# Scores in two visits a unit, meta tokens side by side, another product order in the pair stage of a hybrid mixer block

## The chip, the cores and the metric

The kernel runs on one core of a Trainium2 chip. The metric is the device time of one execution in microseconds, as the median of several runs. A profile of one execution gives the busy time and the waits of each engine: TensorE (PE, with its weight loads as PEld), VectorE (DVE), ScalarE (ACT), GpSimd (POOL) and SyncE (SP), which issues the transfers.

## The reference

A block over 1024 tokens and 16 meta tokens, width 1024, in float32: a pooling mixer and a chunked gated linear attention (gla) side by side, merged by gates, then a squared-ReLU MLP. What the change touches is the projection `z = u @ w_in` and the attention:

```python
z = jnp.einsum('bld,dn->bln', u, w_in)
a, q, k, v, r, lr, ga, gb = jnp.split(z, IN_SPLITS, axis=-1)   # 512, 256, 256, 512, 512, 16, 1024, 1024
...
def gla_chunk_step(S, inp):          # a chunk is 64 tokens, 4 heads, DK 64, DV 128
    qc, kc, vc, ac = inp
    b = jnp.cumsum(ac, axis=2)
    decay = jnp.exp(-jnp.abs(b[:, :, :, None, :] - b[:, :, None, :, :]))
    scores = jnp.einsum('bhtk,bhsk,bhtsk->bhts', qc, kc, decay)
    o = jnp.einsum('bhts,bhsv->bhtv', scores, vc) + jnp.einsum('bhtk,bhkv->bhtv', qc * jnp.exp(b), S)
    ...
```

The 16 meta tokens are a leading partial chunk; their keys and values give the first state S.

## The kernel before

Each float32 operand of a large product is split into a high and a low part (`w1h`, `w1l` of a weight, `th`, `tl` of the tokens), and a product of four row blocks is 12 matmuls: high by high (L300), low by high (L301), high by low (L302). ACT makes the high part (L982), DVE the low one (L983). A float32 matmul shows as one row in the profile if its parts are of the split kind, and as two if both operands are plain float32.

The program runs through stages. The first makes the values v (`v_half`, token blocks t = 0 to 7, and t = 8 for the meta tokens, 16 rows). A second makes the first projections in a written order. The third, `pairs_of_projections`, makes the columns of q, gb, ga and r as 11 pairs of 128 columns, by a scheme with 7 products instead of 8 (P1 to P7). Then come the attention across chunks (`across`), the gated output and the MLP.

A pair's products work on quarter blocks of the weights a11, a12, a21, a22 and sums of them that POOL adds (`fs`, `s3`). P1 and P2 add up in one PSUM bank (the x sum), P5 and P3 in another (the z sum); P6, P7 and P4 have banks of their own (`y`). ACT or DVE read the banks out: P1 to `u2p` (ACT, L1094); P2 to the result of the column by `put`, which is a copy or a tanh on ACT (L942; for gb and ga) and for r a tanh, a scaling (L952) and a product on DVE (L953) that reads the bank too; P6 into `u2p`, P7 into `u3p` and then z + `u3p` (L1102), P4 + `u3p` (L1112), P3 as z + `u2p` (L1116), on DVE. `pairs_order` gives the order of the products: P6 of the pair before, P1, P7 of the pair before, P5, then P4 of the pair before, P2, P3 of the pair before. The x sums lie in turns in the two halves (one bank each) of a wide tile `sc`, and the z sums in two tiles `z`. PE follows the order in which the code is written; the order on DVE and ACT is a scheduler's, and waits between engines are semaphores set by which tile an instruction reads or writes.

Between the products stands the inside of the attention, a generator `insides` that is advanced by a credit: four units (two halves of the tokens, two pairs of heads). A unit (`inside`) loads keys, queries and decays into `gi` and `g`, grows them level by level (`grow`, 5 levels, DVE and ACT), and forms 7 score sets of 16 matmuls of 64x64 (the chunk's own and levels 0 to 5). A burst of those between two products is called a visit here. The scores land in halves of a wide tile `gs` and are laid into `gi` with a mask (`inlay`, L1255); the result is stored to `gi_dram`. In the first half of the tokens each unit is followed by `meta_state`, which turns the decayed meta keys and multiplies them with the meta values (`vm`). In `across`, scores times values (L1449) and queries times states (L1459) are two visits each half, with a small copy between (L1454).

Of the kernel before, what the change touches and what calls it, by code (L numbers as in the profile page):

```python
# [14 lines left out]
P = 128  # L15
# [5 lines left out]
CH = 64  # L21
# [9 lines left out]
MP = 264  # L31
PACE, LEVEL, OPENING, STRETCH = 1.3, 1.6, 6.0, 1.9

# [89 lines left out]
def kernel(  # L123
# [154 lines left out]
    def transposed(u, half, at, tags=("ms",), to=None):  # L278
        rows = u.shape[0]
        th, tl = (t[half] for t in to or (TH, TL))  # L280
        if rows == P:
            for j in range(2):
                turn_n[0] += 1
                b = bank(tags[turn_n[0] % len(tags)]).rearrange("p (a b) -> p a b", a=4)
                for i in range(4):
                    pe.transpose(b[:, i], u[:, (4 * j + i) * P : (4 * j + i + 1) * P], ident)
                split_from_psum(th[:, 4 * j : 4 * j + 4, at : at + P], tl[:, 4 * j : 4 * j + 4, at : at + P], b)
                c = half * HALF + at - OFF[half]
                act.activation(S["xr"][:, 4 * j : 4 * j + 4, c : c + P], b, ACT.Copy)
        else:  # L290
            b = bank("ms")[:, : 8 * rows].rearrange("p (a b) -> p a b", a=8)
            for i in range(8):
                pe.transpose(b[:, i], u[:, i * P : (i + 1) * P], ident[:rows, :rows])
            split_from_psum(th[:, :, at : at + rows], tl[:, :, at : at + rows], b)

# [120 lines left out]
    def v_out(i, t):  # L416

        n = P if t < 8 else META
        b = v_bank.pop((i, t))[:n]
# [9 lines left out]
    def lr_turn():  # L429
# [5 lines left out]
        b = two("y2")[:, 0]  # L435
        pe.transpose(b[:16, :16], S["lrtok"][:16, 8], ident[:16, :16])
        stacked(S["lr"][:, SEQ : SEQ + META], b[:16, :16])
# [155 lines left out]
    def start():  # L593
# [412 lines left out]
    def pairs_order(n_pairs):  # L1006
        yield from (("P1", 0), ("P4", 0), ("P2", 0), ("P5", 0))
        for i in range(1, n_pairs + 1):
            for p in ("P6", "P1", "P7", "P5", "P4", "P2", "P3"):
                n = i if p in ("P1", "P5", "P2") else i - 1  # L1010
                if n < n_pairs and (p, n) != ("P4", 0):
                    yield p, n

    def sums_weights(order, n_pairs, load, eng):

        def tt(out, a, b, op):
            for k in (slice(0, 2), slice(2, 4)) if eng is pool else (slice(0, 4),):
                eng.tensor_tensor(out[:, k], a[:, k], b[:, k], op)

        for p, i in order(n_pairs):  # L1020
# [28 lines left out]
    def first_pair():  # L1049
# [5 lines left out]
        w1_slots()  # L1055
        S["pw"] = sums_weights(pairs_order, len(PAIRS), load_pair, pool)

# [4 lines left out]
    def pairs_of_projections():  # L1062
# [5 lines left out]
        S["u2p"] = right.push("u2p", [P, 2, HALF], F32)  # L1068
        S["u3p"] = right.push("u3p", [P, 2, HALF], F32)
        load(1, 0)  # L1070
        load(1, 1)
        S["N"] = [right.push(f"n{i}", [P, HALF, 2], F32) for i in range(2)]
        S["F"] = right.push("f", [P, HALF, 2], F32)
        S["ends"] = right.push("ends", [P, HALF], F32)
        S["g"] = right.push("g", [P, HALF], F32)
        S["gi"] = right.push("gi", [P, 3, HALF], F32)
        banks(keep=1, y=2, gs=1, z=2)
        x, xb, zb = S["xs"], {}, {}
        total = 7 * len(PAIRS)
        chain, credit = insides(), 0.0  # L1080
        for n, (p, i, (ah, al)) in enumerate(ahead(pair_weights(), 3)):
            bh, bl = x[p]
            if p in ("P1", "P2"):
                b = xb[i] = bank("sc") if p == "P1" else xb[i]
            elif p in ("P5", "P3"):
                b = zb[i] = bank("z") if p == "P5" else zb[i]
# [4 lines left out]
            u2, u3 = S["u2p"][:, i % 2], S["u3p"][:, i % 2]  # L1091
            put, d = PAIRS[i][1:]
            if p == "P1":
                act.activation(u2, b, ACT.Copy)  # L1094
            elif p == "P2":
                put(d, 0, xb.pop(i), None)
            elif p == "P6":
                dve.tensor_tensor(u2, b, u2, ALU.add)
            elif p == "P7":
                dve.tensor_tensor(u3, b, u2, ALU.add)  # L1100
                c = nxt("c")
                dve.tensor_tensor(c, zb[i], u3, ALU.add)  # L1102
# [63 lines left out]

    def meta_state(p):
        pre, suf, y, km = (metab[:, i] for i in (META_LOG[p], 1, 2, 4))
        nc.sync.dma_start(km, k_dram[p, :, :META])
        dve.memset(suf, 0.0)  # L1170
        for m in (1, 2, 4, 8):
            twice(pre, suf, m)
        act.activation(y, suf, ACT.Exp, scale=1.0 / TAU)
        dve.tensor_tensor(y, y, km, ALU.mult)
        yield 5.0
        b = two("gs")[:, 0]
        pe.transpose(b[:META, :P], y, ident)
        kt = gB[32 : 32 + META, 2 * 256 : 2 * 256 + P]
        dve.tensor_copy(kt, b[:META, :P])
        yield 2.0  # L1180
        b = two("gs")[:, 0]
        for e in range(2):
            r = slice(e * CH, (e + 1) * CH)
            pe.matmul(
                b[r, :P], kt[:, r], vm[:, (2 * p + e) * P : (2 * p + e + 1) * P], start=True, stop=True,
                tile_position=(32, e * CH),
            )
        dve.tensor_copy(S["S"][:, 0, p], b[:, :P])
# [19 lines left out]
    def inside(p, half):  # L1208
# [42 lines left out]

        yield 2.0

        def inlay(lvl, b):
            dve.copy_predicated(scc, mask[:, lvl : lvl + 1, None, :].broadcast_to([P, 2, 4, CH]), b)  # L1255

        b = [scores(kq[:, 0], kq[:, 1]), scores(N[0][:, :, 0], N[0][:, :, 1])]
        act.activation(scc, b[0], ACT.Copy)
        inlay(0, b[1])
        e, at = g, 0  # L1260
        for lvl in range(6):
            m, n = 1 << lvl, N[lvl % 2]
            to = at + HALF // (2 * m)
            e2 = ends[:, at:to] if lvl < 5 else dec_of(p, half)
            if lvl < 5:
                grow(m, n, N[1 - lvl % 2], e, e2)
            e2_of, e, at = (e, e2), e2, to
            if lvl < 5:
                yield LEVEL
            if lvl in (1, 3):  # L1270
                b = [scores(N[i][:, :, 0], N[i][:, :, 1]) for i in (1, 0)]
                for i in range(2):
                    inlay(lvl + i, b[i])
            elif lvl == 5:
                b = scores(n[:, :, 0], n[:, :, 1])
                last(n, *e2_of)
                inlay(5, b)
        yield LEVEL
# [137 lines left out]
    def across(p, half):  # L1416
# [533 lines left out]
```

## Time and profile before

| | |
|---|---|
| median of 3 runs | 1198.33 us (1198.26 to 1198.54) |
| profiled execution | 1198.67 us, of which the span from first to last instruction is 1195.8 |
| PE busy | 1182.6 us, 99% |
| DVE, ACT, POOL busy | 853.6, 579.0, 102.1 us |
| first stage (values) | 0 to 72.4 us |
| first projections | 72.4 to 140.7 us |
| pair stage | 140.7 to 376.6 us |
| across chunks | 376.6 to about 460 us |

A row of the profile's timeline reads: start in us, duration in us, engine, line, operation, names (out<-in), shape, count, and in brackets the engine's idle time before it and what ended it. PE's rows overlap: a matmul's duration includes its way through the array, and starts of neighbouring products' matmuls are 0.23 us apart.

### The profile page before, as it was taken

Reading aid. Unit: us, or ns where it says so; the run is one execution under the profiler, and the core shown is the slowest. Engines: PE = TensorE matmul, PEld = TensorE weight load, DVE = VectorE, ACT = ScalarE, POOL = GpSimd, SP = SyncE. Lnnn points to the kernel's source line nnn. Section 1 sums busy time; section 2 is a strip of 40 time slices with the busy share of each in tenths; the row PEclk is TensorE's granted clock in tenths of the full one; section 3 lists DMA queues with packets and bytes.
Section 4 is the critical chain, followed back from the end, with each engine's and each line's share of the span. In section 5 each row is a group of like instructions: output and inputs, shape, how many; then the busy total and the mean of one; then the engine's idle time right before and its main releaser. Section 6 shows DMA issues by size and latency. Waiting matters only on the chain.

```text
span 1195.8 us, 18439 instructions
## 1 busy us (share of the span) xinstructions
PE 1182.6 (99%) x6823; PEld 982.5 (82%) x6823; DVE 853.6 (71%) x1400; ACT 579.0 (48%) x1006; POOL 102.1 (9%) x121
## 2 busy tenths in 40 slices
PE   9999999999999999999999999999999999999997
PEld 7999887777778887888788888888888888888886
DVE  7679657565676779527986766777675887887686
ACT  7566544444456224216754555545454444445454
POOL 0224232333220000000000000000000000000000
PEclk9999999999999999999999999999999999999999
DMA  8232533434357879712254544445389963333532
GB/s 247 69 89 81 180 112 113 143 125 142 124 168 265 293 229 306 257 34 89 89 185 143 165 146 163 153 139 167 132 285 336 328 213 97 97 97 97 168 97 88
DMA packets 151001, 192.79 MB, mean 161 GB/s; under 512 B 12088, under 2 KB 85616, under 8 KB 150912
## 3 DMA queue, kind: packets, MB, share of 16 engines
q1 hardware_dynamic: 150752, 191.56, 50.1%
q8 instruction: 53, 0.87, 0.3%
q14 instruction: 36, 0.29, 0.1%
q10 hardware_dynamic: 160, 0.07, 0.0%
HBM read 128.66 MB, written 62.93 MB: 160 GB/s over the span
## 4 chain that ended last, share of the span: by engine, by line
PE 69%; DVE 3%; issue 1%; ACT 1%; DMA 0%; DVEq 0%
PE b_oa L300 5%; PE b_oa L302 5%; PE b_oa L301 5%; PE b_y L300 4%; PE b_mm L300 4%; PE b_y L301 4%; PE b_y L302 4%; PE b_mm L302 4%; PE b_mm L301 4%; PE b_ob L300 4%; PE b_ob L302 4%; PE b_ob L301 4%; PE b_z L301 3%; PE b_z L300 3%; PE b_z L302 3%; PE b_sc L300 2%
## 5 line engine op out<-in xcount | busy, mean ns | idle before, releaser
L300 PE MATMUL b_z<-th,w1h 128*128 128x512 f32 x240 | 94.3, 393 | 0.0
L301 PE MATMUL b_z<-tl,w1h 128*128 128x512 f32 x240 | 93.6, 390 | 0.4 <-DVE tl L1617 0.4
L302 PE MATMUL b_z<-th,w1l 128*128 128x512 f32 x240 | 93.5, 390 | 0.0
L982 ACT ACTIVATE w1h<-raw 128x512 fp32r<-128x512 f32 x103 | 64.0, 622 | 54.9 <-PE b_y L301 23.1
L300 PE MATMUL b_sc<-th,w1h 128*128 128x512 f32 (+1 forms) x232 | 89.8, 387 | 0.7 <-ACT u2p L1733 0.7
L301 PE MATMUL b_sc<-tl,w1h 128*128 128x512 f32 (+1 forms) x232 | 89.2, 385 | 0.0
L302 PE MATMUL b_sc<-th,w1l 128*128 128x512 f32 (+1 forms) x232 | 89.0, 383 | 0.0
L983 DVE TENSOR_TENSOR w1l<-raw,w1h 128x512 fp32r<-128x512 f32 x103 | 70.6, 686 | 18.4 <-ACT w1h L982 18.4
L982 ACT ACTIVATE w1h<-fs 128x512 fp32r<-128x512 f32 x81 | 51.1, 631 | 65.8 <-PE b_y L301 34.2
L983 DVE TENSOR_TENSOR w1l<-fs,w1h 128x512 fp32r<-128x512 f32 x81 | 56.2, 694 | 21.8 <-ACT w1h L982 21.6
L982 ACT ACTIVATE w1h<-bt 128x512 fp32r<-128x512 f32 x46 | 29.1, 632 | 70.8 <-issue 43.9
L1809 DVE TENSOR_TENSOR bt<-w,w 128x512 f32<-128x512 f32 x80 | 54.6, 683 | 0.6 <-DMA w<-in_w_ff_dram 0.6
L301 PEld LDWEIGHTS b_z<-tl,w1h 128*128 128x128 f32 x240 | 45.1, 188 | 9.9 <-DVE tl L1617 0.8
L300 PEld LDWEIGHTS b_z<-th,w1h 128*128 128x128 f32 x240 | 45.0, 188 | 9.8 <-issue 0.2
L302 PEld LDWEIGHTS b_z<-th,w1l 128*128 128x128 f32 x240 | 45.1, 188 | 9.7
L300 PEld LDWEIGHTS b_sc<-th,w1h 128*128 128x128 f32 x232 | 43.6, 188 | 10.4 <-ACT u2p L1733 1.2
L302 PEld LDWEIGHTS b_sc<-th,w1l 128*128 128x128 f32 x232 | 43.6, 188 | 8.8
L301 PEld LDWEIGHTS b_sc<-tl,w1h 128*128 128x128 f32 x232 | 43.6, 188 | 8.6
L300 PE MATMUL b_mm<-wo,th 128*128 128x512 f32 x128 | 50.4, 393 | 0.0
L983 DVE TENSOR_TENSOR w1l<-bt,w1h 128x512 fp32r<-128x512 f32 x46 | 31.7, 690 | 25.6 <-ACT w1h L982 25.6
L302 PE MATMUL b_mm<-wo,tl 128*128 128x512 f32 x128 | 49.9, 390 | 0.0
L301 PE MATMUL b_mm<-wo,th 128*128 128x512 f32 x128 | 49.8, 389 | 0.0
(535 smaller groups left out, 3405.7 us busy)
## 6 DMA issues: line engine op xcount, KB each, us to landing
hf_dram<-h SPq DMA_DIRECT2D x112, 256.0 KB, 2.1
raw<-hf_dram SPq DMA_DIRECT2D x112, 256.0 KB, 2.7
w<-in_w_ff_dram SPq DMA_DIRECT2D x64, 256.0 KB, 4.6
raw<-in_w_in_dram SPq DMA_DIRECT2D x18, 512.0 KB, 4.8
raw<-in_w_ff_dram SPq DMA_DIRECT2D x16, 512.0 KB, 4.2
rawx<-in_w_ff_dram SPq DMA_DIRECT2D x16, 512.0 KB, 4.1
rawp<-in_w_in_dram SPq DMA_DIRECT2D x14, 512.0 KB, 4.8
xs<-in_x_dram SPq DMA_DIRECT2D x8, 512.0 KB, 5.4
```

Source lines behind the costliest of these rows:

```text
L300: pe.matmul(ps, ah, bh, start=first and i == 0, stop=False, skip_group_check=more)
L301: pe.matmul(ps, ah, bl, start=False, stop=False, skip_group_check=more)
L302: pe.matmul(ps, al, bh, start=False, stop=last and i == n - 1, skip_group_check=more)
L982: act.activation(hi, a, ACT.Copy)
L983: dve.tensor_tensor(lo, a, f32(hi), ALU.subtract)
L1809: dve.tensor_tensor(bt, w, S["w2"][q[3:]][:, i], ALU.add if q[2] == "+" else ALU.subtract)
```

## The change

1. *Meta tokens.* A new tile `mz` holds the high and low parts of the 16 meta tokens side by side as 32 rows. For t = 8 two matmuls a row block (by `vw` high and low) replace three. The 32 rows are kept, and products with them sum both; `lr`'s transpose becomes two matmuls with parts of the identity.
2. *Scores.* A unit has two visits in place of four: own, 0, 1, 2 after level 1's growth, and 3, 4, 5 at the end. There is a second wide tile `g2` for them and a third `N` tile; the wide tile `g2` takes the PSUM of the two `z` tiles.
3. *Meta states* of both pairs of heads are one step behind the first half's units.
4. *Across.* The pause between scores times values and queries times states becomes zero, which joins the two visits.
5. *Pair order.* P6, P1, P5, P7, P4, P2, P3, with only P1 and P2 from the next pair. The x sum is half 0 of `sc` and the z sum half 1, `u3p` is single, and the first P4 is kept in `g`. POOL's sums are regrouped by that order.

```diff
-        if tag in ("sc", "gs"):
+        if tag in ("sc", "gs", "g2"):
...
+        elif t == 8:
+            for k in range(4 * j, 4 * j + 4):
+                for w in range(2):
+                    pe.matmul(b, S["mz"][:, k], vw[:, w, k], start=k + w == 0, stop=k + w == KT)
...
-        yield from (("P1", 0), ("P4", 0), ("P2", 0), ("P5", 0))
+        yield from (("P1", 0), ("P4", 0), ("P2", 0))
         for i in range(1, n_pairs + 1):
-            for p in ("P6", "P1", "P7", "P5", "P4", "P2", "P3"):
-                n = i if p in ("P1", "P5", "P2") else i - 1
+            for p in ("P6", "P1", "P5", "P7", "P4", "P2", "P3"):
+                n = i if p in ("P1", "P2") else i - 1
...
-        banks(keep=1, y=2, gs=1, z=2)
-        x, xb, zb = S["xs"], {}, {}
+        banks(keep=1, y=2, gs=1, g2=1)
+        x, xb, zb = S["xs"], two("sc")[:, 0], two("sc")[:, 1]
...
-            if p in ("P1", "P2"):
-                b = xb[i] = bank("sc") if p == "P1" else xb[i]
-            elif p in ("P5", "P3"):
-                b = zb[i] = bank("z") if p == "P5" else zb[i]
-            else:
-                b = bank("y")
+            b = xb if p in ("P1", "P2") else zb if p in ("P5", "P3") else bank("y")
...
-    def meta_state(p):
+    def meta_states():
...
-    def scores(kk, qq):
-        turn_n[0] += 1
-        c = (turn_n[0] % 2) * 4 * CH
-        b = two("gs")[:, :, c : c + 4 * CH].rearrange("p e (j t) -> p e j t", j=4)
+    def scores(place, kk, qq):
+        c = (place % 2) * 4 * CH
+        b = two("g2" if place > 1 else "gs")[:, :, c : c + 4 * CH].rearrange("p e (j t) -> p e j t", j=4)
...
+            if lvl == 1:
+                own = scores(0, kq[:, 0], kq[:, 1])
+                for n in range(3):
+                    b[n] = scores(1 + n, N[n][:, :, 0], N[n][:, :, 1])
+                act.activation(scc, own, ACT.Copy)
+        for n in range(3):
+            b[3 + n] = scores(n, N[n][:, :, 0], N[n][:, :, 1])
+        last(N[2], e, dec_of(p, half))
+        for n in range(3, 6):
+            inlay(n, b.pop(n))
...
-        yield 5.0
+        yield 5.8
...
         dve.tensor_copy(rms[p][:, :2], o[:, :, 3, P - 1])
-        yield 0.8
+        yield 0.0
```

What the program's order makes of it, at three places. Line numbers shift with the change (L300 to L302 become L303 to L305, L982 becomes L993, L1094 becomes L1126, L1200 becomes L1236). `b_sc`, `b_z`, `b_y`, `b_gs`, `b_g` are PSUM tiles; `th`, `tl`, `t0h` and so on are parts of the tokens; in brackets stands which engine's semaphore an instruction waits for.

PE at the end of P1 and the start of the product behind it, early in the pair stage. Before, P7 comes behind P1:

```order
L300 MATMUL b_sc<-th_132,w1h 128x512
L301 MATMUL b_sc<-tl_136,w1h 128x512
L302 MATMUL b_sc<-th_132,w1l 128x512
L300 MATMUL b_y<-t1h,w1h 128x512
L301 MATMUL b_y<-t1l,w1h 128x512
L302 MATMUL b_y<-t1h,w1l 128x512 [waits DVE_49]
```

After, P5 comes behind P1 (P3 behind P2 reads alike, with its first row waiting for ACT):

```order
L303 MATMUL b_sc<-th_132,w1h 128x512
L304 MATMUL b_sc<-tl_136,w1h 128x512
L305 MATMUL b_sc<-th_132,w1l 128x512
L303 MATMUL b_sc<-th_140,w1h 128x512 [waits Activation_49]
L304 MATMUL b_sc<-tl_144,w1h 128x512
L305 MATMUL b_sc<-th_140,w1l 128x512 [waits DVE_49]
```

P5 writes the other half of the tile that P1 has written, and its first matmul waits for ACT; the count that it waits for is that of the copy of P1's half to `u2p`.

ACT around that copy. Before:

```order
L982 ACTIVATE w1h<-fs 128x512 [waits PE_49,Activation_49,Pool_49]
L947 ACTIVATE c<-c 128x512 [waits DVE_49]
L982 ACTIVATE w1h<-raw_120 128x512 [waits PE_49,Activation_49]
L982 ACTIVATE w1h<-rawp_989 128x512 [waits PE_49,Activation_49]
L1094 ACTIVATE u2p<-b_sc 128x512 [waits PE_49]
```

After, in a unit of the attention:

```order
L993 ACTIVATE w1h<-raw_120 128x512 [waits PE_49]
L1272 ACTIVATE n_1728<-f 128x64x8 [waits DVE_49]
L993 ACTIVATE w1h<-rawp_980 128x512 [waits PE_49]
L1126 ACTIVATE u2p<-b_sc 128x512 [waits PE_49]
L993 ACTIVATE w1h<-fs 128x512 [waits PE_49]
L993 ACTIVATE w1h<-fs 128x512 [waits PE_49,Activation_49,Pool_49]
```

In both a split of weights, which waits for PE, stands directly ahead of the copy to `u2p`.

PE at a unit's visit. Before, the second visit of a unit (two score sets):

```order
L302 MATMUL b_z<-th_140,w1l 128x512
L1200 MATMUL b_gs<-n_1732 64x64 x16
L1200 MATMUL b_gs<-n_1728 64x64 x16
L300 MATMUL b_y<-t0h,w1h 128x512
L301 MATMUL b_y<-t0l,w1h 128x512
```

After, the first visit of a unit (four score sets), between P2 and P3:

```order
L305 MATMUL b_sc<-th_132,w1l 128x512
L1236 MATMUL b_gs<-gi 64x64 x16
L1236 MATMUL b_gs<-n_1720 64x64 x16
L1236 MATMUL b_g_2074<-n_1724 64x64 x16
L1236 MATMUL b_g_2074<-n_1728 64x64 x16
L303 MATMUL b_sc<-th_140,w1h 128x512
```

Four score sets stand in one burst, over two wide tiles.

More of the change, by code (lines that the diff above doesn't have):

```diff
@@ L31 @@
 MP = 264
-PACE, LEVEL, OPENING, STRETCH = 1.3, 1.6, 6.0, 1.9
+PACE, OPENING, STRETCH = 1.3, 6.0, 1.9
 class Stack:
@@ L293, in transposed @@
                 pe.transpose(b[:, i], u[:, i * P : (i + 1) * P], ident[:rows, :rows])
-            split_from_psum(th[:, :, at : at + rows], tl[:, :, at : at + rows], b)
+            h, l = th[:, :, at : at + rows], tl[:, :, at : at + rows]
+            split_from_psum(h, l, b)
+            act.activation(S["mz"][:, :, :META], f32(h), ACT.Copy)
+            act.activation(S["mz"][:, :, META:], f32(l), ACT.Copy)
     def mm3(ps, n, lhs, rhs, first=True, last=True, more=False):
@@ L393, in halves @@
         return [slice(h * HALF, (h + 1) * HALF) for h in range(2)]
-    vm = gB[32 : 32 + META, : 2 * 256]
+    vm = gB[32 : 32 + 2 * META, : 2 * 256]
     v_bank = {}
@@ L401, in v_half @@
         vw, w = S["vw"][i], 256 + 16 * (i == 1)
-        half, n = (t // 4, P) if t < 8 else (0, META)
-        at = OFF[half] + (t % 4) * P if t < 8 else 0
+        half, n = t // 4, P if t < 8 else 2 * META
+        at = OFF[half % 2] + (t % 4) * P
         if j == 0:
@@ L416, in v_out @@
     def v_out(i, t):
-        n = P if t < 8 else META
+        n = P if t < 8 else 2 * META
         b = v_bank.pop((i, t))[:n]
@@ L435, in lr_turn @@
         b = two("y2")[:, 0]
-        pe.transpose(b[:16, :16], S["lrtok"][:16, 8], ident[:16, :16])
+        for u in range(2):
+            pe.matmul(
+                b[:16, :16], S["lrtok"][:32, 8], ident[:32, u * 16 : (u + 1) * 16], start=u == 0, stop=u == 1
+            )
         stacked(S["lr"][:, SEQ : SEQ + META], b[:16, :16])
@@ L601, in start @@
         S["vw"] = [right.push(f"vw{i}", [P, 2, KT, n], F32R) for i, n in enumerate((256, VP))]
+        S["mz"] = right.push("mz", [P, KT, 2 * META], F32R)
         buffer("vo", 3, 2 * P, right)
@@ L1006, in pairs_order, with pair_sums @@
     def pairs_order(n_pairs):
-        yield from (("P1", 0), ("P4", 0), ("P2", 0), ("P5", 0))
+        yield from (("P1", 0), ("P4", 0), ("P2", 0))
         for i in range(1, n_pairs + 1):
-            for p in ("P6", "P1", "P7", "P5", "P4", "P2", "P3"):
-                n = i if p in ("P1", "P5", "P2") else i - 1
+            for p in ("P6", "P1", "P5", "P7", "P4", "P2", "P3"):
+                n = i if p in ("P1", "P2") else i - 1
                 if n < n_pairs and (p, n) != ("P4", 0):
                     yield p, n
+    def pair_sums(n_pairs, load):
+        for p, i in pairs_order(n_pairs):
+            a11, a12 = (w1raw[i, 0][:, k : k + 4] for k in (0, 4))
+            if p in ("P1", "P2"):
+                s = a11 if p == "P1" else a12
+            else:
+                a21, a22 = (w1raw[i, 1][:, k : k + 4] for k in (0, 4))
+                if p != "P4":
+                    f, s3 = quad(S["fs"][:, i % 2]), quad(S["s3"])
+                if p == "P6":
+                    s = f
+                    in_halves(s3, a21, a22, ALU.add)
+                    in_halves(f, s3, a11, ALU.subtract)
+                elif p == "P5":
+                    s = s3
+                elif p == "P7":
+                    s = s3
+                    in_halves(s3, a11, a21, ALU.subtract)
+                elif p == "P3":
+                    s = f
+                    in_halves(f, a12, f, ALU.subtract)
+                else:
+                    s = a22
+            yield p, i, split(s)
+            if p == "P3" and i + 2 < n_pairs:
+                load(i + 2, 0)
+                load(i + 2, 1)
     def sums_weights(order, n_pairs, load, eng):
-        def tt(out, a, b, op):
-            for k in (slice(0, 2), slice(2, 4)) if eng is pool else (slice(0, 4),):
-                eng.tensor_tensor(out[:, k], a[:, k], b[:, k], op)
+        tt = eng.tensor_tensor
         for p, i in order(n_pairs):
@@ L1055, in first_pair @@
         w1_slots()
-        S["pw"] = sums_weights(pairs_order, len(PAIRS), load_pair, pool)
+        S["pw"] = pair_sums(len(PAIRS), load_pair)
     def pair_weights():
@@ L1068, in pairs_of_projections @@
         S["u2p"] = right.push("u2p", [P, 2, HALF], F32)
-        S["u3p"] = right.push("u3p", [P, 2, HALF], F32)
+        S["u3p"] = right.push("u3p", [P, HALF], F32)
         load(1, 0)
         load(1, 1)
-        S["N"] = [right.push(f"n{i}", [P, HALF, 2], F32) for i in range(2)]
+        S["N"] = [right.push(f"n{i}", [P, HALF, 2], F32) for i in range(3)]
         S["F"] = right.push("f", [P, HALF, 2], F32)
-        S["ends"] = right.push("ends", [P, HALF], F32)
+        S["ends"] = right.push("ends", [P, 384], F32)
         S["g"] = right.push("g", [P, HALF], F32)
         S["gi"] = right.push("gi", [P, 3, HALF], F32)
-        banks(keep=1, y=2, gs=1, z=2)
-        x, xb, zb = S["xs"], {}, {}
+        banks(keep=1, y=2, gs=1, g2=1)
+        x, xb, zb = S["xs"], two("sc")[:, 0], two("sc")[:, 1]
         total = 7 * len(PAIRS)
@@ L1082, in pairs_of_projections @@
             bh, bl = x[p]
-            if p in ("P1", "P2"):
-                b = xb[i] = bank("sc") if p == "P1" else xb[i]
-            elif p in ("P5", "P3"):
-                b = zb[i] = bank("z") if p == "P5" else zb[i]
-            else:
-                b = bank("y")
+            b = xb if p in ("P1", "P2") else zb if p in ("P5", "P3") else bank("y")
             more = p in ("P2", "P3")
             mm3(b, 4, lambda k: (ah[:, k], al[:, k]), lambda k: (bh[:, k], bl[:, k]), first=not more, more=more)
-            u2, u3 = S["u2p"][:, i % 2], S["u3p"][:, i % 2]
+            u2, u3 = S["u2p"][:, i % 2], S["u3p"]
             put, d = PAIRS[i][1:]
@@ L1095, in pairs_of_projections @@
             elif p == "P2":
-                put(d, 0, xb.pop(i), None)
+                put(d, 0, xb, None)
             elif p == "P6":
@@ L1101, in pairs_of_projections @@
                 c = nxt("c")
-                dve.tensor_tensor(c, zb[i], u3, ALU.add)
+                dve.tensor_tensor(c, zb, u3, ALU.add)
                 put(d + 1, 1, c, c)
@@ L1105, in pairs_of_projections @@
                     c = nxt("c")
-                    dve.tensor_tensor(c, S["ends"], u3, ALU.add)
+                    dve.tensor_tensor(c, S["g"], u3, ALU.add)
                     put(d + 1, 0, c, c)
             elif p == "P4" and i == 0:
-                act.activation(S["ends"], b, ACT.Copy)
+                act.activation(S["g"], b, ACT.Copy)
             elif p == "P4":
@@ L1115, in pairs_of_projections @@
                 c = nxt("c")
-                dve.tensor_tensor(c, zb.pop(i), u2, ALU.add)
+                dve.tensor_tensor(c, zb, u2, ALU.add)
                 put(d, 1, c, c)
@@ L1165, in twice @@
         dve.tensor_tensor(pv[:, :, 1], pv[:, :, 1], end(0), ALU.add)
-    def meta_state(p):
[L1168 to L1174, printed above, removed]
+    def meta_states():
+        y, yy = [metab[:, i] for i in (2, 5)], [S["g"][:, 160 + 32 * i : 192 + 32 * i].rearrange("p (a t) -> p a t", a=2) for i in range(2)]
+        for p in range(2):
+            pre, suf, km = (metab[:, i] for i in (META_LOG[p], 1, 4))
+            nc.sync.dma_start(km, k_dram[p, :, :META])
+            dve.memset(suf, 0.0)
+            for m in (1, 2, 4, 8):
+                twice(pre, suf, m)
+            act.activation(y[p], suf, ACT.Exp, scale=1.0 / TAU)
+            dve.tensor_tensor(
+                yy[p], *(a[:, None, :].broadcast_to([P, 2, META]) for a in (y[p], km)), ALU.mult
+            )
@@ L1175, in meta_state @@
         yield 5.0
         b = two("gs")[:, 0]
[L1177 to L1180, printed above, removed]
-        b = two("gs")[:, 0]
[L1182 to L1187, printed above, removed]
@@ L1188, in meta_state @@
-        dve.tensor_copy(S["S"][:, 0, p], b[:, :P])
+        for p in range(2):
+            pe.transpose(b[: 2 * META, p * P : (p + 1) * P], yy[p].rearrange("p a t -> p (a t)"), ident)
+        kt = gB[32 : 32 + 2 * META, 2 * 256 : 2 * 256 + 2 * P]
+        dve.tensor_copy(kt, b[: 2 * META, : 2 * P])
+        yield 3.0
+        b = two("gs")[:, 0]
+        for p in range(2):
+            for e in range(2):
+                n = 2 * p + e
+                pe.matmul(
+                    b[e * CH : (e + 1) * CH, p * P : (p + 1) * P], kt[:, n * CH : (n + 1) * CH],
+                    vm[:, n * P : (n + 1) * P], start=True, stop=True, tile_position=(32, e * CH),
+                )
@@ L1219, in inside @@
         nc.sync.dma_start(g, decay_dram[p, half])
-        yield 4.5
+        yield 4.0
         pairs = lambda a: a.rearrange("p (b u) n -> p b u n", u=2)
@@ L1250, in last @@
             dve.tensor_tensor(e2, ev[:, :, 0], ev[:, :, 1], ALU.mult)
-        yield 2.0
+        yield 1.0
         def inlay(lvl, b):
             dve.copy_predicated(scc, mask[:, lvl : lvl + 1, None, :].broadcast_to([P, 2, 4, CH]), b)
[L1257 to L1278, printed above, removed]
+        e, b = g, {}
+        for lvl in range(5):
+            e2 = (ends[:, :256], g[:, :128], ends[:, 256:320], g[:, 128:160], ends[:, 320:336])[lvl]
+            grow(1 << lvl, N[lvl % 3], N[(lvl + 1) % 3], e, e2)
+            e = e2
+            if lvl > 1:
+                inlay(lvl - 2, b.pop(lvl - 2))
+            yield (1.4, 1.6, 2.0, 2.0, 2.4)[lvl]
+            if lvl == 1:
[8 more added lines that the diff above has]
+            inlay(n, b.pop(n))
+        yield 1.6
         nc.sync.dma_start(gi_dram[p, half], gi)
@@ L1284, in insides @@
                 yield from inside(p, half)
-                if half == 0:
-                    yield from meta_state(p)
+            if half == 0:
+                yield from meta_states()
     step(one, pairs_of_projections)
```

1 line of the change is left out of this document (added).

## The prediction

> **What bounds the kernel now.** I read the totals of the page first, then the table of stages, then the list of what TensorE (PE) waited for.
>
> ```profile
> span 1195.8 us, 18439 instructions
> PE 1182.6 (99%) x6823; PEld 982.5 (82%) x6823; DVE 853.6 (71%) x1400; ACT 579.0 (48%) x1006; POOL 102.1 (9%) x121
> PEclk9999999999999999999999999999999999999999
> 140.70:376.60 235.90, 234.37 (x1831) 187.60 (x1830) 152.66 (x250) 111.64 (x183) 67.89 (x82) 1.00 0.46 141
> 376.60:460.00 83.40, 82.94 (x767) 66.57 (x766) 61.91 (x123) 25.19 (x35) 0.00 (x0) 1.00 0.85 277
> PE b_ms L495 <- POOL xr L480: 1.5, 1, 1.5
> PE b_gs L1200 <- DVE gi L1255: 0.9, 2, 0.7
> PE b_gs L1200 <- ACT gi L1249: 0.5, 1, 0.5
> ```
>
> PE is busy for 99% of the span at full clock. In the pair stage (140.70 to 376.60) it is busy 234.37 of 235.90 us, and the list of waits knows few, each short. So PE is the bound everywhere, and every microsecond that it gains or loses is one of the total. Two things can change the time: the PE work itself, and new waits of PE. There is nearly no slack in which a new wait could vanish.
>
> **The change part by part.** The sum stands against the profiled execution, 1198.67 us (span 1195.8 and 2.9 around it); the median of the runs shown, 1198.33, is 0.34 less.
>
> *Meta tokens side by side.* The values of the 16 meta tokens are the last 48 products of the first stage.
>
> ```profile
> 66.68 0.28 PE L300 MATMUL b_mm<-vw,th 128*16 128x256 f32 x1
> 72.30 0.28 PE L302 MATMUL b_mm<-vw,tl 128*16 128x272 f32 x1
> ```
>
> From the first to the last are 47 steps in 5.62 us, 0.120 each. 32 are left of 48: 16 x 0.120 = -1.9 us. One small transpose becomes two small matmuls, and ACT gets two copies; I allow +0.15 for the first, nothing for the copies (ACT is busy 48%; uncovered they would cost about one copy). Sum -1.75.
>
> *Fewer visits.* A "visit" is a burst of 64-row matmuls between two products. Its price comes from the products on both sides. PE's matmuls there start 0.23 apart.
>
> ```profile
> 195.82 0.39 PE L302 MATMUL b_sc<-th,w1l 128*128 128x512 f32 x1
> 196.08 0.63 ACT L982 ACTIVATE w1h<-raw 128x512 fp32r<-128x512 f32 x1 [2.21 <-PE b_sc L301]
> 196.14 1.19 PE L1200 MATMUL b_gs<-n 64*64 64x64 f32 x64
> 196.62 0.58 ACT L1094 ACTIVATE u2p<-b_sc 128x512 f32<-128x512 f32 x1
> 197.26 0.50 PE L300 MATMUL b_y<-t1h,w1h 128*128 128x512 f32 x1
> 197.60 0.39 PE L301 MATMUL b_y<-t1l,w1h 128*128 128x512 f32 x1
> ```
>
> Without the visit the next product would have begun at 195.82 + 0.23 = 196.05; its second matmul at 197.60 puts its effective start at 197.37. The visit cost 1.32 us. Its 64 instructions fill 1.19 less one instruction's own latency (0.22), so 0.97 to 1.0; about 0.33 is the price of the visit itself. Each of four units goes from four visits to two: 8 x 0.33 = -2.65. The values and queries visits of the later stage merge, two fewer: -0.65 (the copy between them lies behind the other pair's 32 instructions).
>
> The Trainium skill, "TensorEngine Tiling (Array Packing)", section Key Properties, says that a switch of the tiling mode drains the array. The 0.33 agrees, and the sum is the same by it.
>
> The meta states:
>
> ```profile
> 220.45 0.39 PE L302 MATMUL b_y<-t1h,w1l 128*128 128x512 f32 x1
> 220.77 0.43 PE L1184 MATMUL b_gs<-gB 16*64 16x128 f32 x4
> 221.47 0.39 PE L301 MATMUL b_z<-tl,w1h 128*128 128x512 f32 x1
> ```
>
> By the same reckoning this visit of 4 instructions costs 0.56. Two become one with twice the matmuls: -0.5.
>
> *Waits of the last visit of a unit.*
>
> ```profile
> 254.72 0.74 DVE L1255 COPY_PREDICATED gi<-mask,b_gs 128x512 f32<-128x512 uint8 x1
> 255.44 0.39 PE L302 MATMUL b_z<-th,w1l 128*128 128x512 f32 x1
> 255.68 0.72 DVE L1255 COPY_PREDICATED gi<-mask,b_gs 128x512 f32<-128x512 uint8 x1
> 256.55 0.71 PE L1200 MATMUL b_gs<-n 64*64 64x64 f32 x32 [0.72 <-DVE gi L1255]
> 312.60 0.71 PE L1200 MATMUL b_gs<-n 64*64 64x64 f32 x32 [0.55 <-ACT gi L1249]
> ```
>
> These visits have no place in the new order: -0.78, -0.6, and -0.2 for the other DVE wait of the list. Sum -1.6.
>
> All gains: 1.75 + 2.65 + 0.65 + 0.5 + 1.6 = 7.15 us.
>
> *The order of the products.* This row decides the case. The visit at 256.55 is score 5, which writes the half of the wide tile that score 3 had. Score 3's half was read by 255.46 (254.72 + 0.74). Yet PE stood until the other half had been read too, at 255.68 + 0.72 = 256.40. So halves of a wide tile are guarded as one tile. Before, this touches one tile and a few visits. In the new order the x sum (P1, P2) and the z sum (P5, P3) are the two halves of the one tile `sc`, and P5 stands right behind P1, P3 right behind P2. Each must wait until ACT has emptied the half just finished. The order of the changed program shows it: the first `b_sc` row of P5 and that of P3 wait for ACT, where the row behind P1 waited for nothing before, and ACT has a weight split ahead of its reading.
>
> Price: in the rows above P1's last matmul would have been followed at 196.05; ACT splits weights until 196.71, and has read P1 at 196.62 + 0.58 = 197.20. That is 1.15 us behind the boundary. P2:
>
> ```profile
> 186.21 0.39 PE L302 MATMUL b_sc<-th,w1l 128*128 128x512 f32 x1
> 186.47 0.63 ACT L982 ACTIVATE w1h<-s 128x512 fp32r<-128x512 f32 x1 [1.26 <-PE b_sc L301]
> 187.01 0.58 ACT L942 ACTIVATE t<-b_sc 128x512 f32<-128x512 f32 x1
> 578.15 0.57 ACT L1733 ACTIVATE u2p<-b_sc 128x512 f32<-128x512 f32 x1
> 578.78 0.50 PE L300 MATMUL b_sc<-th,w1h 128*128 128x512 f32 x1 [0.25 <-ACT u2p L1733]
> 579.11 0.39 PE L301 MATMUL b_sc<-tl,w1h 128*128 128x512 f32 x1
> ```
>
> Again 187.59 - 186.44 = 1.15. The last three rows, from a later stage, show PE's restart behind such a reading: 578.72 to 578.78 is 0.06, and its second matmul comes 0.33 later instead of 0.23, 0.1 more. So 1.15 + 0.06 + 0.1 = 1.3 us for each stall.
>
> Count: 10 steps P1 to P5 and 10 steps P2 to P3. Three have a score visit between (over 1.15 us, hidden), one the state visit (0.57, which leaves 0.75). Two P2 belong to the r columns, whose sum is read last by DVE:
>
> ```profile
> 340.76 0.39 PE L302 MATMUL b_sc<-th,w1l 128*128 128x512 f32 x1
> 341.50 0.58 ACT L942 ACTIVATE t<-b_sc 128x512 f32<-128x512 f32 x1
> 342.11 0.82 ACT L952 ACTIVATE t<-t,small 128x512 f32<-128x512 f32 x1
> 342.96 0.69 DVE L953 TENSOR_TENSOR c<-b_sc,t 128x512 f32<-128x512 f32 x1
> ```
>
> 343.65 - 340.99 = 2.66, with the restart 2.8 each. The remaining 14 cost 1.3: 14 x 1.3 + 0.75 + 2 x 2.8 = 24.55.
>
> Two smaller ones. The second pair's P2 now follows P7 of the first and waits for the sum over `z`:
>
> ```profile
> 159.91 0.40 PE L302 MATMUL b_y<-t1h,w1l 128*128 128x512 f32 x1
> 161.55 0.68 DVE L1102 TENSOR_TENSOR c<-b_z,u3p 128x512 f32<-128x512 f32 x1
> 214.03 0.83 DVE L1224 TENSOR_TENSOR n<-gi,g 128x512 f32<-128x512 f32 x1 [3.19 <-DMA gi<-q_dram]
> 326.15 0.83 DVE L1224 TENSOR_TENSOR n<-gi,g 128x512 f32<-128x512 f32 x1 [3.03 <-DMA gi<-q_dram]
> ```
>
> 162.23 - 160.14 = 2.1, with the restart +2.25. And DVE stands about 3 us at a unit's start for the loads of `gi`, on one queue with the store of the unit before. The emptying of P7 or P3 stands behind that in DVE's order, and P1 and P2 now need the half that it frees. With three such starts behind other work, nothing is lost if the loads are early, and about 8 us if all wait the full 3 with little cover; I take 4, the middle.
>
> Losses: 24.55 + 2.25 + 4 = 30.8; net +23.65 on 1198.67 is 1222.3, or 1222 on the median.
>
> **The rivals.**
> *Halves apart.* If P5 needn't wait for P1's reading, only the gains are left: 1198.3 - 7.15 = 1191. For it: only one engine reads a half, and P5 writes another bank. Against it: the whole-tile wait at 256.55. It decides if ACT's reading ends before the boundary, and the rows put it 1.15 us behind. The Trainium skill, "PSUM — Partial Sum Buffer", section PSUM bank collisions, asks for guards by bank and quadrant only; by that rule the wait isn't needed and the time is that of this rival, but the row at 256.55 shows a wait wider than the rule.
> *Short stalls.* ACT reads the sum ahead of the split, or the splits are early because PE stands more often. Then a stall is 0.58 + 0.16, about 0.75, r 2.0, and the loads cost nothing: 14 x 0.75 + 0.2 + 4 + 1 = 15.7, net +8.5, 1207. Against it: the split waits for the very product that ends (2.21 <-PE b_sc), so it starts at the boundary and is first in ACT's order.
> *A backlog on top.* PE stands, DVE waits for loads, ACT's order holds growth copies ahead of the reading. The 14 stalls grow to 1.5, r to 3.5, the loads take 8: 21 + 0.75 + 7 + 2.25 + 8 = 39, net +32, 1230. For it: DVE is the fullest engine beside PE in the pair stage (152.66 of 235.90).
> *The clock.* PE's longest wait in this trace is 1.5 us, with the clock at 9 in each slice. The Trainium skill, "TensorE: Matmul & The Clock Gate", section Part 1, halves the clock after an idle window of about 3.4 us; the r stalls of 2.8 would come near. No run here shows it; if each were followed by as long a stretch at half speed it would add an estimated 3.4 us.
>
> **How the numbers follow.** Halves apart 5%, short stalls 13%, my forecast 65%, backlog 15%, the clock 2%. My forecast's own spread is the price of a stall, 1.15 to 1.4, and the loads at 0 to 8: +18 to +29. The range goes down to 1208 (short stalls) and up to 1231 (backlog), which leaves out halves apart, half of the short stalls and a part of the backlog, some 2 in 10. What a measurement can tell here is about 0.2%, 2.4 us. Faster 6% (halves apart, and a little of mixed cases), same 1%, slower 93%.
>
> **What the profile after would show.** PE's list of waits gets two long entries at the products, `b_sc` behind ACT `u2p` and behind ACT `t`, some 10 to 12 us each, with single waits near 1.2, and entries behind DVE `c`. In the pair stage PE's busy time falls by about 4 us while the stage grows by 26 to 28; the first stage is 1.9 shorter, the later one 0.7, and the stages behind unchanged. Each unit shows two bursts of 128 and 96 instructions without a wait. If no waits at `b_sc` appear, the argument is wrong at its main step; if they are near 0.6, the order of ACT is misjudged.

## The result: 1231.95 us, slower by 2.8%

The changed kernel took 1231.95 us (median of 4 runs, 1231.53 to 1232.98), the kernel before on the same chip 1198.3 (1198.12 to 1198.54). The ratio is 1.0281, with a 95% interval of 1.0269 to 1.0293. The forecast was 1222, with a range to 1231; the time lies just outside it.

The totals of the page, the two rows of the table of stages, and PE's list of waits, of the kernel after. In the table the column before the transfers' share is the granted clock; in the list stand the total, the number and the longest wait in us.

```profile
span 1230.2 us, 18404 instructions
PE 1189.3 (97%) x6810; PEld 985.5 (80%) x6810; DVE 857.0 (70%) x1398; ACT 579.3 (47%) x1008; POOL 104.3 (8%) x121
140.70:376.60 235.90, 211.26 (x1701) 166.37 (x1700) 135.75 (x221) 93.11 (x157) 67.45 (x79) 0.97 0.40 122
PE b_sc L303 <- ACT u2p L1126: 11.3, 8, 3.3
PE b_sc L303 <- ACT t L953: 9.1, 7, 3.0
PE b_sc L303 <- DVE c L964: 6.0, 2, 3.4
PE b_sc L303 <- DVE c L1134: 2.6, 2, 2.4
```

The waits are those that were forecast, in kind and number: 8 behind `u2p` (P1 to P5, one of them behind the state visit), 7 behind `t` (P2 to P3), 2 behind the r product on DVE, 2 of P2 behind the sum over z. They add up to 29.0 us. But the clock in these 236 us is 0.97, where it was 1.00 before.

An ordinary stall, P1 to P5, on PE and ACT:

```profile
176.15 0.39 PE L305 MATMUL b_sc<-th,w1l 128*128 128x512 f32 x1
176.41 0.63 ACT L993 ACTIVATE w1h<-rawp 128x512 fp32r<-128x512 f32 x1 [2.17 <-PE b_sc L304]
176.94 0.58 ACT L1126 ACTIVATE u2p<-b_sc 128x512 f32<-128x512 f32 x1
177.57 0.50 PE L303 MATMUL b_sc<-th,w1h 128*128 128x512 f32 x1 [1.04 <-ACT u2p L1126]
177.91 0.40 PE L304 MATMUL b_sc<-tl,w1h 128*128 128x512 f32 x1
```

The split, then the reading, end at 177.52; PE starts at 177.57 in place of 176.38, and its next matmul is 0.34 later in place of 0.23. That is 1.30 us, the 1.3 of the forecast. A long one, P1 to P5 later on:

```profile
346.45 0.39 PE L305 MATMUL b_sc<-th,w1l 128*128 128x512 f32 x1
348.28 0.76 ACT L1285 ACTIVATE gi<-f 128x256 f32<-128x256 f32 x2 [1.81 <-DVE f L1273]
348.94 0.62 ACT L993 ACTIVATE w1h<-raw 128x512 fp32r<-128x512 f32 x1
349.46 0.58 ACT L1126 ACTIVATE u2p<-b_sc 128x512 f32<-128x512 f32 x1
350.09 0.60 PE L303 MATMUL b_sc<-th,w1h 128*128 128x512 f32 x1 [3.25 <-ACT u2p L1126]
350.49 0.63 PE L304 MATMUL b_sc<-tl,w1h 128*128 128x512 f32 x1
350.92 0.63 PE L305 MATMUL b_sc<-th,w1l 128*128 128x512 f32 x1
```

Two things are new here. In ACT's order a copy of the unit stands ahead of the split and the reading, and waits itself for DVE (1.81), so the stall is 3.5 and not 1.3. And behind it the matmuls start 0.427 apart (350.49 to 350.92) in place of 0.228, for 3.4 us: the clock has halved. The same happens behind each of the five waits of 2.4 us and more. Five windows around them, with a clock between 0.83 and 0.89 (the second number is PE's busy time):

```profile
160.00:170.00 10.00, 6.66 (x21) 5.02 (x22) 6.23 (x10) 3.35 (x6) 3.63 (x4) 0.83 0.34 105
235.00:250.00 15.00, 12.03 (x45) 9.38 (x45) 8.64 (x15) 5.99 (x11) 4.21 (x6) 0.89 0.29 87
352.00:358.00 6.00, 6.00 (x56) 4.64 (x59) 1.16 (x2) 1.24 (x2) 0.00 (x0) 0.85 0.00 0
364.00:378.00 14.00, 11.00 (x40) 8.21 (x38) 4.61 (x7) 5.47 (x9) 4.72 (x6) 0.88 0.56 187
387.00:400.00 13.00, 9.60 (x35) 7.37 (x34) 7.80 (x11) 8.24 (x12) 2.05 (x3) 0.87 0.16 62
```

Summed over PE's rows from start to start (all that exceeds 0.228 between two matmuls of a product), the 19 stalls cost 31.9 us, their slower restarts 19 x 0.11 = 2.1, and the matmuls at half speed 7.9 (33 of them at 0.427 and some on the edge). Losses are thus 41.9; the span grew by 34.4, which leaves 7.5 of gains.

### The profile page after: what moved, and what is told of

Its sections match the earlier page's. It is cut to its first block, busy times and chain, and to the rows that moved or that the text cites. A ratio compares the mean times of both kernels' runs of the same rounds, so it can differ in the third digit from the quotient of the medians.

```text
span 1230.2 us, 18404 instructions
## 1 busy us (share of the span) xinstructions
PE 1189.3 (97%) x6810; PEld 985.5 (80%) x6810; DVE 857.0 (70%) x1398; ACT 579.3 (47%) x1008; POOL 104.3 (8%) x121
## 4 chain that ended last, share of the span: by engine, by line
PE 75%; DVE 5%; ACT 2%; DMA 2%; issue 2%; SPq 0%; DVEq 0%; ACTq 0%
PE b_sc L303 5%; PE b_y L303 5%; PE b_y L304 5%; PE b_y L305 5%; PE b_sc L304 5%; PE b_oa L303 5%; PE b_oa L305 5%; PE b_oa L304 5%; PE b_sc L305 4%; PE b_mm L303 4%; PE b_mm L305 4%; PE b_mm L304 4%; PE b_ob L303 4%; PE b_ob L305 4%; PE b_ob L304 4%; PE b_z L303 2%
## 5 line engine op out<-in xcount | busy, mean ns | idle before, releaser
L303 PE MATMUL b_sc<-th,w1h 128*128 128x512 f32 (+1 forms) x320 | 129.2, 404 | 29.4 <-ACT u2p L1126 11.3
L304 PE MATMUL b_sc<-tl,w1h 128*128 128x512 f32 (+1 forms) x320 | 126.7, 396 | 0.0
L305 PE MATMUL b_sc<-th,w1l 128*128 128x512 f32 (+1 forms) x320 | 126.1, 394 | 0.0
L303 PEld LDWEIGHTS b_sc<-th,w1h 128*128 128x128 f32 x320 | 61.8, 193 | 50.4 <-ACT u2p L1126 14.6
L993 ACT ACTIVATE w1h<-raw 128x512 fp32r<-128x512 f32 x103 | 64.0, 622 | 48.9 <-PE b_sc L304 20.7
L993 ACT ACTIVATE w1h<-fs 128x512 fp32r<-128x512 f32 x70 | 44.2, 632 | 79.1 <-PE b_y L304 38.0
L305 PEld LDWEIGHTS b_sc<-th,w1l 128*128 128x128 f32 x320 | 62.1, 194 | 13.2
L993 ACT ACTIVATE w1h<-bt 128x512 fp32r<-128x512 f32 x46 | 29.1, 632 | 70.9 <-issue 43.9
L304 PE MATMUL b_z<-tl,w1h 128*128 128x512 f32 x152 | 59.3, 390 | 0.4 <-DVE tl L1650 0.4
L303 PE MATMUL b_z<-th,w1h 128*128 128x512 f32 x152 | 59.3, 390 | 0.2 <-DVE h L1783 0.2
L305 PE MATMUL b_z<-th,w1l 128*128 128x512 f32 x152 | 59.2, 390 | 0.0
L303 PE MATMUL b_mm<-wo,th 128*128 128x512 f32 x128 | 50.4, 393 | 0.0
L305 PE MATMUL b_mm<-wo,tl 128*128 128x512 f32 x128 | 49.9, 390 | 0.0
L303 PE MATMUL b_y<-wo,w1h 128*128 128x512 f32 x128 | 49.8, 389 | 0.0
L304 PE MATMUL b_y<-wo,w1h 128*128 128x512 f32 x128 | 49.8, 389 | 0.0
L305 PE MATMUL b_y<-wo,w1l 128*128 128x512 f32 x128 | 49.8, 389 | 0.0
```

What stands on the lines that cost most here:

```text
L303: pe.matmul(ps, ah, bh, start=first and i == 0, stop=False, skip_group_check=more)
L304: pe.matmul(ps, ah, bl, start=False, stop=False, skip_group_check=more)
L305: pe.matmul(ps, al, bh, start=False, stop=last and i == n - 1, skip_group_check=more)
L993: act.activation(hi, a, ACT.Copy)
```

## The experiments

My theory after the result: the waits come from the shared wide tile (34.0 us; the expectation below has 34.6 for the same stalls), the slow matmuls from the clock that falls when PE stands idle (7.9), and the two longest plain stalls from ACT's order. The rivals: the new order is too tight whatever the tiles; the slow matmuls have a cause of their own; DVE's backlog, not ACT's order, sets the long stalls. The first four kernels ran on one chip, where the kernel before took 1197.63; the last three on another, where it took 1197.73.

**The two sums in tiles of their own.**

```diff
-        banks(keep=1, y=2, gs=1, g2=1)
-        x, xb, zb = S["xs"], two("sc")[:, 0], two("sc")[:, 1]
+        banks(keep=0, xb=1, zb=1, y=2, gs=1, g2=1)
+        x, xb, zb = S["xs"], bank("xb"), bank("zb")
...
-        banks(keep=1, mm=4, m2=1)
+        banks(keep=0, sc=1, mm=4, m2=1)
```

> The changed kernel, with the x sum and the z sum in two tiles of one bank each in place of the two halves of one tile; all else as changed. If the waits of the changed kernel (34.6 us in 19 stalls by its trace, and 8 us of slower matmuls behind the five longest) come from the shared tile, nearly all of them go: 1232 - 34.6 - 8.0 = 1189.4, allowing a little for waits that take their place, 1189 to 1193, faster than before by 0.5 to 0.7%. Rival: the new order itself is too tight (weights or sums of the products are not ready, ACT or DVE too late); then PE waits elsewhere, and the time stays above 1205.

Measured: 1190.92 us (1190.41 to 1191.87), ratio to before 0.9945 (0.9932 to 0.9957): faster than both kernels. PE's and POOL's instructions and their order are those of the changed kernel. On ACT and DVE the scheduler's order differs in some places, but that is not what removes the waits: P5 now starts 0.23 behind P1's last matmul, while ACT reads P1 only 2.4 us later.

```profile
170.26 0.39 PE L305 MATMUL b_xb<-th,w1l 128*128 128x512 f32 x1
170.49 0.40 PE L303 MATMUL b_zb<-th,w1h 128*128 128x512 f32 x1
172.88 0.58 ACT L1126 ACTIVATE u2p<-b_xb 128x512 f32<-128x512 f32 x1
```

One wait is left behind these products, at the second pair's beginning. There P3 adds to the bank that DVE is reading, so this wait belongs to the data and not to the tile:

```profile
PE b_zb L303 <- DVE c L1134: 0.8, 1, 0.8
core 0: 1189.1 us, clock 0.999
```

This shows the main step: the halves of the wide tile `sc`, a bank each, are guarded as one. Without the waits that follow from it the change gains 6.7 us; with them, and with the slower matmuls behind them, it loses 33.65. The rival that the order is too tight has fallen.

**Extra matmuls in the five longest stalls.** They write a spare bank that nobody reads.

```diff
+            if (p, i) in (("P2", 1), ("P3", 3), ("P5", 8), ("P3", 8), ("P3", 9)):
+                idle = bank("y")
+                for k in range(8):
+                    pe.matmul(idle, ah[:, k % 4], bh[:, k % 4], start=True, stop=True)
             mm3(b, 4, ...)
```

> The changed kernel, with 8 extra matmuls (1.8 us) into a spare bank ahead of the five products that wait longest (2.4 to 3.4 us), so that PE idles for 0.6 to 1.6 us there in place of 2.4 to 3.4. Their results are read by nobody. If the slow matmuls behind these stalls (about 40 at 0.427 in place of 0.228 us) come from the clock falling after PE stood idle, the stalls last as long as before, the granted clock is 1.00 throughout, and the time is 1232 - 8 = 1224 (1223 to 1225.5). Rival: the slow matmuls have another cause, such as a contended memory or weights that come late behind a stall; then nothing is gained, 1231 to 1233.

Measured: 1223.24 us (1222.72 to 1223.97), ratio 1.0213 (1.0199 to 1.0227). One such stall, which lasted 3.36 from row to row in the changed kernel (237.83 to 241.19), and the clock around it:

```profile
235.69 0.39 PE L305 MATMUL b_sc<-th,w1l 128*128 128x512 f32 x1
235.91 1.99 PE L1125 MATMUL b_y<-th,w1h 128*128 128x512 f32 x8
239.03 0.50 PE L303 MATMUL b_sc<-th,w1h 128*128 128x512 f32 x1 [1.13 <-ACT t L953]
239.37 0.40 PE L304 MATMUL b_sc<-tl,w1h 128*128 128x512 f32 x1
235.00:250.00 15.00, 13.87 (x149) 10.99 (x148) 8.30 (x15) 6.15 (x12) 4.72 (x6) 1.00 0.42 123
```

The stall is as long as it was (235.69 to 239.03, 3.34), but PE idles for 1.13 of it, the clock stays at 1.00 and the matmuls behind it start 0.23 apart. Work that nobody needs has made the kernel faster by 1.0213 against 1.0281, about 8 us. So the clock's part is shown, by its size too.

**Three extra matmuls in place of eight.** The same edit with `range(3)`.

> As the kernel with 8 extra matmuls, but with 3 (0.7 us): PE idles for about 1.7, 1.9, 2.3, 2.6 and 2.7 us in the five places. If the clock falls after an idle time of about 2.2 us, the two shorter ones are cured and three slow stretches are left: 1232 - 3.2 = 1229. If it takes an idle time near a whole window of about 3.4 us, as the Trainium skill, TensorE: Matmul & The Clock Gate, Part 1, has it, none is left: 1224. If any idle time over 1.7 us does it, all are left: 1232.

Measured: 1228.96 us (1227.19 to 1231.6), ratio 1.026 (1.0246 to 1.0274). The median fits the first of the three expectations, but the runs differ by as much as three slow stretches, and the profiled one shows that no single idle time decides:

```profile
222.97 0.50 PE L303 MATMUL b_sc<-th,w1h 128*128 128x512 f32 x1 [1.84 <-ACT u2p L1130]
...
224.16 0.63 PE L304 MATMUL b_sc<-tl,w1h 128*128 128x512 f32 x1
...
367.43 0.50 PE L303 MATMUL b_sc<-th,w1h 128*128 128x512 f32 x1 [1.92 <-DVE c L964]
367.76 0.39 PE L304 MATMUL b_sc<-tl,w1h 128*128 128x512 f32 x1
```

Behind a wait of 1.84 us the matmuls became slow 1.2 us after the restart; behind one of 1.92 they did not. Waits of 2.26, 2.56 and 2.73 in that run were followed by slow matmuls.

The traces show what decides instead. All slow stretches of a trace begin on one grid of 3.413 us: in the changed kernel at 162.62, 241.12, 350.35, 367.42 and 394.73, which are 23, 32, 5 and 8 steps apart. A stretch follows a step in which PE was busy for less than about half. For the two waits of this run, the step with the wait and the step behind it:

```profile
220.42:223.83 3.41, 1.57 (x8) 0.96 (x7) 3.41 (x5) 1.63 (x3) 2.62 (x3) 1.00 0.07 10
223.83:227.24 3.41, 3.41 (x10) 2.65 (x9) 2.06 (x9) 0.00 (x0) 0.00 (x0) 0.50 0.54 146
363.78:367.19 3.41, 1.72 (x8) 1.08 (x6) 1.20 (x2) 1.93 (x3) 1.07 (x2) 1.00 0.95 360
367.19:370.61 3.42, 3.18 (x14) 2.64 (x15) 0.31 (x2) 0.29 (x1) 0.34 (x1) 1.00 0.66 207
```

The wait of 1.84 lies whole in one step, which is busy for 0.46 of its length; that of 1.92 is cut by the grid, and its step is busy for 0.50. In the changed kernel the steps ahead of the five stretches are busy for 0.08 to 0.40, all other steps of the pair stage for 0.60 or more. With eight extra matmuls no step is below 0.53, and no stretch follows.

**The unit's last copies on POOL.**

```diff
-                act.activation(o[:, :, 1 - u], f[:, :, 1 - u], ACT.Copy)
+                pool.tensor_copy(o[:, :, 1 - u], f[:, :, 1 - u])
```

> The changed kernel, with the two plain copies at the end of each unit (gi from f) on POOL in place of ACT. In the changed kernel's trace two stalls last 3.0 and 3.3 us where such a copy, which waits for DVE, stands in ACT's order ahead of the reading of the finished sum. If ACT's order is the cause, these two shrink to 1.0 to 1.2, and the slower matmuls behind them go too: 1232 - 1.9 - 2.2 - 3.1 = 1224.8 (1224 to 1227). Rival: DVE's backlog is the cause and ACT waits for it in any case: 1230 to 1232.

Measured: 1226.63 us (1226.21 to 1228.99), ratio 1.0245 (1.0231 to 1.0259). The two stalls, in that kernel:

```profile
239.72 0.50 PE L303 MATMUL b_sc<-th,w1h 128*128 128x512 f32 x1 [1.96 <-ACT t L953]
344.93 0.50 PE L303 MATMUL b_sc<-th,w1h 128*128 128x512 f32 x1 [1.04 <-ACT u2p L1126]
```

The second fell from 3.25 to 1.04, as expected, and ACT's order is its cause. The first fell only from 2.97 to 1.96. What holds ACT there for another microsecond stands in the same trace: the tanh of another result column, ahead of the split and the reading, which waits for P4's sum on DVE.

```profile
237.33 0.67 DVE L1144 TENSOR_TENSOR c<-b_y,u3p 128x512 f32<-128x512 f32 x1
238.03 0.63 ACT L953 ACTIVATE t<-c 128x512 f32<-128x512 f32 x1 [0.61 <-DVE c L1144]
```

DVE works without a pause from 233.04 on, mostly at the unit's growth and masks, so at this stall the rival holds in part: ACT's order sets which rows stand ahead, and DVE's backlog how late they come. Neither stall had a slow stretch behind it.

**The r sums copied first.**

```diff
-        t, o, g = half_tanh(b), o or nxt("c"), gnorm[:, h : h + 1]
+        if o is None:
+            o = nxt("c")
+            act.activation(o, b, ACT.Copy)
+            b = o
+        t, g = half_tanh(b), gnorm[:, h : h + 1]
```

> The changed kernel, with the x sum of the two r pairs first copied to SBUF by ACT; tanh, scaling and product then read the copy. If the wait of P3 there lasts until the last reader of the tile (DVE's product, 2.6 and 3.4 us of wait), the copy shortens it to about 1.0 and 1.0 to 1.8, and the clock does not fall behind these two: 1232 - 1.6 - 2.0 - 3.1 = 1225.3 (1224.5 to 1227). If the clock has nothing to do with it, 1228.4. If ACT, with one more instruction a pair, is late elsewhere, no gain: 1231 to 1233.

Measured: 1226.09 us (1224.67 to 1229.29), ratio 1.0238 (1.0224 to 1.0252). Both waits are shorter, and the clock did not fall behind them:

```profile
PE b_sc L303 <- ACT c L964: 2.2, 2, 1.1
370.08 0.50 PE L303 MATMUL b_sc<-th,w1h 128*128 128x512 f32 x1 [1.04 <-ACT c L964]
```

6.0 us of waits in two became 2.2. In the profiled run the wait behind the state visit was longer than in the changed kernel (2.41 in place of 1.74), and a slow stretch of two steps followed it. This run, at 1229.29, is the slowest of the four.

**The visits of the later stage undone**, on top of the two tiles (the pauses 5.0 and 0.8 again).

> The kernel with the two sums in tiles of their own, with the pauses of the later stage as before the change, so that scores times values and queries times states are two visits again in each half. By the price of a visit (0.33 us) it is 0.65 us slower than the kernel with the sums apart, 1191.6; rival: the copy between the two products makes PE wait in the merged visit, then it is equal or faster, 1190.5 to 1191.

Measured: 1192.04 us (1191.39 to 1192.78), 1.1 above the kernel with the tiles apart, each with about 0.7 of spread and on different chips. The intervals of the two ratios to before overlap, so the times alone do not tell the two kernels apart. The traces have it closer: from product to product the merged visit costs 3.85 us, the two apart 2.11 each, 0.37 saved in each half.

**P1's sum read by DVE.**

```diff
-                act.activation(u2, b, ACT.Copy)
+                dve.tensor_copy(u2, b)
```

> The changed kernel, with P1's sum read by DVE in place of ACT. If the 1.3 us of an ordinary stall behind P1 are the rest of ACT's weight split and then the reading, a reading by a DVE that is free lasts 0.68, and the stall 0.85: six ordinary stalls save 0.45 each, 1232 - 2.7 = 1229.3. Rival: DVE is fuller than ACT in this stage and has rows of growth ahead of the reading; then the stalls grow, some over 2 us with slower matmuls behind them, 1233 to 1245.

Measured: 1238.95 us (1236.07 to 1241.74), ratio 1.0346 (1.0328 to 1.0363): the rival held. PE's list, and the worst place with what DVE does ahead of it:

```profile
PE b_sc L303 <- DVE u2p L1126: 15.4, 8, 3.7
224.78 0.39 PE L305 MATMUL b_sc<-th,w1l 128*128 128x512 f32 x1
226.36 1.21 DVE L1271 TENSOR_TENSOR n<-n,ends 128x512 f32<-128x512 f32 x1
227.49 0.68 DVE L1273 TENSOR_TENSOR f<-n,ends 128x512 f32<-128x512 f32 x1
228.09 0.68 DVE L1126 COPY u2p<-b_sc 128x512 f32<-128x512 f32 x1
228.82 0.80 PE L303 MATMUL b_sc<-th,w1h 128*128 128x512 f32 x1 [3.65 <-DVE u2p L1126]
```

Growth of the unit stands ahead of the reading. In two places, where DVE was free, the wait was 0.78, where ACT's was 0.98 and 1.04. So the price of an ordinary stall fits what the forecast added it up from; but an engine that is filled with other work is a worse reader.

## Why the prediction was wrong

**Right.** What bounds the kernel; the main step that the two halves are guarded as one tile, shown by the kernel with the tiles apart; the count of 20 steps and of those that a visit covers; the ordinary stall, 12 of them at 1.31 on the average against 1.3; the direction. The gains: the rows show 7.5 us against 7.15. The kernel with the tiles apart agrees: it gains 6.7, with one wait of 0.8 left. The visits of the pair stage cost 22.4 us before and 17.4 now (wait behind the state visit apart), 5.0 less against 4.75; the meta values

```profile
66.77 4.12 PE L416 MATMUL b_mm<-vw,mz 128*32 128x256 f32 x32
70.72 0.29 PE L303 MATMUL b_sc<-th,w1h 128*128 128x264 f32 x1
```

end 1.70 earlier than the 72.42 that followed from 72.30 before, against 1.9, and the later visits are 0.73 shorter against 0.65.

**Right, with a wrong reason.** The prediction took the guard from the wait at 256.55, where one set of scores waited for the reading of another half of the wide tile `gs`. That row cannot tell a guard by tile from one by bank. Each score set covers 256 columns in both banks of `gs` (`two("gs")[:, :, c : c + 4 * CH]`), so the two halves share their banks, and a guard by bank would have made PE wait too. The halves of `sc` are a bank each. That P5 would wait was shown by the changed program's order alone, and by the result and the kernel with the tiles apart.

**The step that failed: the clock.** The forecast's sum has no term for it. It stood among the rivals with a chance of 2%, and with 3.4 us, worked out from the two r stalls alone. It cost 7.9 us, since five waits and not two set it off. The forecast took from the Trainium skill, "TensorE: Matmul & The Clock Gate", section Part 1, that an idle window of about 3.4 us is needed, and found none that long. The waits that were followed by half speed here were 2.41, 2.97, 3.25, 2.61 and 3.40 us long, so waits well below it were enough. The Trainium skill, "TensorE: Matmul & The Clock Gate", section Part 1, also says that the window runs freely, and gives the warm-up as a window of 3.4 us; the slow stretches of 3.4 us and their grid agree with that. With 7.9 us the forecast sum would have been 1230.

**Terms that were mis-sized.** The span grew by 34.4 us against a net 23.65: 7.9 more by the clock, 3.2 by the stalls, 0.35 less by the gains. The stalls cost 34.0 us against 30.8. Two of the 14 plain ones were not plain: ACT's order held a unit's copy (and at the first a tanh too) ahead of the reading, each waiting for DVE, and they cost 3.2 and 3.5 us, 4.1 more than 2 x 1.3. The prediction named this as a backlog and priced it as 0.2 on every stall, where it falls on two. The r stalls were 2.9 and 3.7 against 2.8 each, P2 of the second pair 2.7 against 2.25, and the remainder behind the state visit 1.85 against 0.75. The loads, for which 4 stood in the sum, cost some 0.5 at one P2 and at most the 1.1 of excess behind the state visit. There DVE's row waited 2.09 for `g`, and ACT's order has a growth copy, which waits for DVE, ahead of the reading:

```profile
272.33 0.83 DVE L1260 TENSOR_TENSOR n<-gi,g 128x512 f32<-128x512 f32 x1 [2.09 <-DMA g<-decay_dram]
276.38 0.50 PE L303 MATMUL b_sc<-th,w1h 128*128 128x512 f32 x1 [1.74 <-ACT u2p L1126]
```

So 2.4 us too many for the loads hid a part of the 4 us too few for the two long stalls, and the backlog rival (1230) came nearest in time, for another reason than its own.

**Left open.** Where exactly the edge lies: steps that were busy for 0.47 (P1's sum read by DVE, a wait of 2.42) and 0.50 had no slow stretch behind them, while one of 0.52 (the r sums copied, a wait of 2.41, with the state visit in the step) had one. The profile models the ends of matmuls, so these shares are rough. Where the grid lies in runs without a profile is not on record; it may be why the runs with three extra matmuls differ.

## What to carry to other kernels

Where an accumulator is moved into the half of a larger tile, look which instructions now name the same tile: the wait follows the tile, not the bank that is written, and a first matmul that waits for another engine where none did before is a stall at every turn of the loop. Give what is written by turns a tile of its own; here that alone was worth about 40 us. And where PE is busy all the time, price a stall that can leave a step of 3.4 us less than half busy twice: once for the wait, and once for the slower matmuls behind it.

## What the runs showed that I had not expected

The granted clock halves for a stretch of 3.413 us (matmuls 0.427 apart in place of 0.228) behind waits well below that length. No length of one wait decides it: a wait of 1.84 us had a slow stretch behind it and one of 1.92 had none, one of 2.12 had one (the copies on POOL) and one of 2.42 had none (P1's sum read by DVE). All 22 slow stretches in the pair stages of these traces begin on their trace's grid of 3.413 us, behind a step in which PE was busy for 0.08 to 0.52 of the time. So a stretch may begin with the restart or more than a microsecond later (matmuls slow from 394.92 on behind the longest wait, which ended at 393.35). Some last for two steps (13 matmuls behind a wait of 2.73); there PE stood idle for the first 0.69 us or more of the first slow step too. Eight matmuls that nobody needs, put into a stall that is there anyway, keep the clock up and were worth about 8 us in five places.
